# Two conv FFNs with one 512-column matmul for the high half of a weight chunk, matmuls on zeros at the start, and another order of the first loads

## The chip, the cores and the metric

The kernel runs on one core of one Trainium2 chip. The metric is the device time of one execution in microseconds (us). Three runs of the kernel before took 1246.49, 1248.91 and 1246.49 us; the median is 1246.49 us. The execution that was profiled took 1248.71 us.

## The reference, cut to what matters

Two blocks run one after the other on 256 tokens of width 1024, in float32, with one batch row. The first block has two SwiGLU FFNs (width 2816) around a mixer and a gated embedding at its end; the second has two layers, each a mixer and a convolutional FFN. The change bears on the two convolutional FFNs:

```
def conv_ffn(u, w_up, conv_w, conv_b, w_down):
    hdn = causal_dwconv(u @ w_up, conv_w) + conv_b
    gate, val = jnp.split(hdn, 2, axis=-1)
    return (jax.nn.silu(gate) * val) @ w_down
```

Here `w_up` is 1024 x 5632, `w_down` is 2816 x 1024, and the convolution is causal over three tokens and separate for each channel. The norms before and after it, the mixers and the first block stay as they are.

## The kernel before, in words

**Arithmetic.** Every large product is made from three products in the fp32r format. A weight `raw` that DMA has brought is split into `hi` (ScalarE, a copy that rounds) and `lo` (VectorE, the difference of `raw` and `hi`); the activations are split in the same way into `xh` and `xl`. The product is `hi*xh + hi*xl + lo*xh`, added up in PSUM.

**Tiling.** Weights come in halves of a chunk, 128 x 1024 values (512 KB) each, through three `raw` buffers and six `hi` and six `lo` buffers (`halves`, lines 584 to 606). An FFN has 11 groups of 256 inner channels. The up product of nearly all groups is made by `row_units` (line 713): the weight is the stationary operand and the moving one is the activations of all 256 tokens, 8 steps of 128 inner rows for each half of a chunk. In a convolutional FFN the first group of a layer goes another way (`col_units`); the other ten have two chunks each, of two halves: ten groups x 2 x 2 x 8 is 320 steps in a layer, 640 in both. The two halves of a chunk (gate and value channels) share one PSUM bank of 512 columns. The down product of a group takes the weights as the moving operand, 512 columns at a time, and adds up in four banks that stay in use over the whole layer. So four of the eight PSUM banks are left for the up products.

**What follows an up product** (`up_fin`, line 1627): ScalarE scales each half from PSUM and adds the bias, VectorE adds the two shifted taps straight from PSUM, then ScalarE makes the silu, GpSimd the product, and ScalarE and VectorE split it for the down product.

**Order.** The code first records all operations (`Plan`, lines 67 to 371) and then lists them with a planner, which lays them out in time by a table of assumed costs: forward passes place operations by priority, and a backward pass between two forward passes makes new priorities. `ITERS` is the number of forward passes, of which the one with the shortest planned end is used; `bias` moves an operation's priority by hand, and `LB` says how much of that is kept for the later passes. Every engine then works off its list in that order. All DMA goes through SyncE's queue (SP).

The steps of the prediction touch `row_units`, `up_fin`, `halves`, `xt` (line 631), `consts` (line 528) and `run` (line 1691).

Of the kernel before, what the change touches and what calls it, by code (L numbers as in the profile page):

```python
# [14 lines left out]
P = 128  # L15
# [8 lines left out]
LEAD = 2  # L24
RING = 6
# [8 lines left out]
ITERS = 2  # L34
# [6 lines left out]
LB = 0.2  # L41
# [332 lines left out]
class Kern:  # L374
    def __init__(self, plan, a, tap):
        self.plan, self.nc, self.a, self.tap = plan, plan.nc, a, tap
        self.phase = 0
        self.pieces = PIECES

# [48 lines left out]
    def tt(self, out, a, b, op, eng="DVE"):  # L428
        n = self.fsz(out)

        def way(eng):
            if op == ALU.pow:
                c = 360 + 165 * n
            else:
                c = 114 + 2.13 * n if eng == "POOL" else 69 + 1.04 * n + self.part(out)
            return eng, c, lambda: self.ew(eng).tensor_tensor(out=out, in0=a, in1=b, op=op), op != ALU.pow and not self.ps_(a, b)  # L436
        self.plan.add([way(x) for x in eng.split("|")], [out], [a, b])

# [89 lines left out]
    def consts(self):  # L528
# [7 lines left out]
        self.plan.bias = -2e6  # L536
# [47 lines left out]
    def halves(self, src, idx, width, gain_k=None):  # L584

        def prep(h):
# [3 lines left out]
            for j in range(np_):  # L590
                z = slice(j * hw // np_, (j + 1) * hw // np_)
                self.dma(raw[:, z], src[idx][:, h * hw:(h + 1) * hw][:, z])
# [38 lines left out]
    def xt(self):  # L631
        xh = self.plan.tile("xh", [P, KD, S], F32R, 2)
        xl = self.plan.tile("xl", [P, KD, S], F32R, 2)
        return xh, xl
# [77 lines left out]

    def row_units(self, src, c0, xh, xl, fin):

        box = {}
        units = []
        for hf, prep in enumerate(self.halves(src, c0, 2048)):
            def run(prep=prep, hf=hf):
                hi, lo = prep()
                if hf == 0:  # L720
                    box["ps"] = self.psum("m").rearrange("p (c t) -> p c t", c=2)
                o = box["ps"][:, hf, :]
                for k in range(KD):
                    wh, wl = hi[:, 128 * k:128 * k + 128], lo[:, 128 * k:128 * k + 128]
                    self.mms([(o, wh, xh[:, k, :], k == 0, False), (o, wh, xl[:, k, :], False, False),
                              (o, wl, xh[:, k, :], False, k == KD - 1)])
                if hf == 1:
                    fin(box["ps"])
            units.append(run)
        return units  # L730


    def ffn(self, src, na, xh, xl, rs, fin):
# [21 lines left out]
        def row_fin(i):  # L755
            def f(ps):
# [8 lines left out]
                self.tt(gu, ps, rb, ALU.mult)  # L765
# [25 lines left out]
        for g in range(NG + 1):  # L791
            if g < na:
                self.run_units(self.col_units(src, up_at[g], 512, xh, xl, tok_fin(g)))
            elif g < NG:
                for c in range(2):
                    for run in self.row_units(src, up_at[g] + c, xh, xl, row_fin(2 * g + c)):
                        run()
            if g > 0:
                self.run_units(down(g - 1), lead=2 if g == NG else 0)
# [822 lines left out]
    def conv_ffn(self, layer, xh, xl, fin):  # L1622
# [4 lines left out]
        def up_fin(i):  # L1627
            def f(ps):
                tm = self.big("cv").rearrange("p (c t) -> p c t", c=2)
                ws = [lambda j, c=c: cw[:, j, 2 * i + c:2 * i + c + 1] for c in range(2)]  # L1630
                for c, w in enumerate(ws):
                    self.act(tm[:, c], ps[:, c], AF.Identity, bias=w(3), scale=w(2))
                for c, w in enumerate(ws):
                    self.stt(tm[:, c, 1:], ps[:, c, :S - 1], w(1), tm[:, c, 1:], ALU.mult, ALU.add)
                    self.stt(tm[:, c, 2:], ps[:, c, :S - 2], w(0), tm[:, c, 2:], ALU.mult, ALU.add)
# [40 lines left out]
        for g in range(NG + 1):  # L1676
# [3 lines left out]
            elif g < NG:  # L1680
                for i in (2 * g, 2 * g + 1):
                    for run in self.row_units(a[f"cf_u{layer}"], i, xh, xl, up_fin(i)):
                        run()
            if g > 0:
                if g < NG:
                    self.run_units(down(g - 1), lead=0)
                else:
                    self.run_units(down(g - 1), lead=2)


    def run(self):
# [6 lines left out]
        for i in range(4):  # L1698
            for z in ([slice(0, 256), slice(256, 512)] if i == 0 else [slice(0, 512)]):
                self.plan.bias = -1e6 if i == 0 and z.start == 0 else 0  # L1700
# [228 lines left out]
```

## Time and profile before

| | |
|---|---|
| median of three runs | 1246.49 us |
| the profiled execution | 1248.71 us |
| its span (first to last instruction) | 1246.9 us |
| TensorE matmuls busy | 1218.3 us, 8084 instructions |
| VectorE busy | 857.1 us |
| ScalarE busy | 672.4 us |
| GpSimd busy | 194.5 us |

Matmuls are pipelined: each row gives a duration of 0.28 us (256 columns), although the next one starts 0.12 us later. So what a matmul costs is read from the distance of the starts, and a busy TensorE isn't yet one at its peak. The names are output <- moving operand, stationary operand: `psa<-xh,hi` is the high activations against the high weights. Line 513 is the helper that issues nearly all matmuls, 436 and 451 the VectorE helpers, 470 and 477 the ScalarE ones.

### The profile page before, as it was taken

How to read it: one execution, taken by the hardware profiler on the slowest of the kernel's cores; microseconds unless marked ns; L12 is line 12 of the kernel's file. 1: busy time of each engine (PE TensorE's matmuls, PEld its weight loads, DVE VectorE, ACT ScalarE, POOL GpSimd, SP SyncE). 2: the span in 40 equal slices, each digit the busy share in tenths (PEclk: the TensorE clock that was granted, in tenths of full speed). 3: DMA queues.
4: the chain of work that ended last, by engine and by line, in shares of the span. 5: the costliest groups of instructions: out<-in, count | busy, mean ns of one | idle time of the engine just before them, and what ended most of it. 6: DMA issues, size and time to landing. Idle time of an engine off the chain costs nothing.

```text
span 1246.9 us, 21305 instructions
## 1 busy us (share of the span) xinstructions
PE 1218.3 (98%) x8084; PEld 1101.0 (88%) x8084; DVE 857.1 (69%) x1627; ACT 672.4 (54%) x1125; POOL 194.5 (16%) x247
## 2 busy tenths in 40 slices
PE   7999999999999999999999999999999999999997
PEld 7899998787899999789998799999799887999996
DVE  5665567876755655778687786776868557766776
ACT  5444445764654444557465675555652356655554
POOL 2111010420011111002001011111113521111111
PEclk9999999999999999999999999999999999999999
DMA  8755554425455555552424555555553244555552
GB/s 282 231 185 176 189 180 148 143 94 194 161 181 188 187 183 192 180 165 78 146 75 150 195 174 185 181 196 181 187 190 103 80 158 155 185 179 193 187 194 93
DMA packets 61158, 209.61 MB, mean 168 GB/s; under 512 B 7424, under 2 KB 9728, under 8 KB 60928
## 3 DMA queue, kind: packets, MB, share of 16 engines
q1 hardware_dynamic: 61056, 208.26, 50.6%
q8 instruction: 63, 1.03, 0.3%
q14 instruction: 39, 0.32, 0.1%
HBM read 207.18 MB, written 1.05 MB: 167 GB/s over the span
## 4 chain that ended last, share of the span: by engine, by line
PE 79%; DVE 7%; DMA 5%; ACT 4%; issue 2%; POOL 1%; SPq 0%; DVEq 0%; POOLq 0%; ACTq 0%
PE psa L513 77%; DVE lo L436 3%; ACT hi L470 2%; DMA raw<-in_w_ffn 2%; PE psa L524 2%; DVE big L451 1%; DMA raw<-in_cf_u 1%; DVE big L436 1%; POOL sml L436 1%; ACT big L470 1%; DMA raw<-in_w_out 1%; DMA big<-in_xT 1%; ACT L366 1%; DVE xl L436 0%; DVE c_h L451 0%
## 5 line engine op out<-in xcount | busy, mean ns | idle before, releaser
L436 DVE TENSOR_TENSOR lo<-raw,hi 128x512 fp32r<-128x512 f32 x756 | 506.9, 715 | 244.0 <-ACT hi L470 240.7
L470 ACT ACTIVATE hi<-raw 128x1024 fp32r<-128x1024 f32 x381 | 394.0, 1047 | 336.1 <-PE psa L513 237.1
L513 PE MATMUL psa<-xh,hi 128*128 128x256 f32 x1568 | 448.6, 286 | 7.3 <-ACT hi L470 7.0
L513 PE MATMUL psa<-xh,lo 128*128 128x256 f32 x1568 | 445.3, 284 | 1.3 <-DVE lo L436 1.0
L513 PE MATMUL psa<-xl,hi 128*128 128x256 f32 x1568 | 443.7, 283 | 0.1
L513 PEld LDWEIGHTS psa<-xh,hi 128*128 128x128 f32 x1568 | 298.8, 191 | 16.8 <-ACT hi L470 7.4
L513 PEld LDWEIGHTS psa<-xl,hi 128*128 128x128 f32 x1568 | 298.6, 190 | 9.5 <-DVE xl L436 0.4
L513 PEld LDWEIGHTS psa<-xh,lo 128*128 128x128 f32 x1568 | 298.4, 190 | 3.2 <-DVE lo L436 3.1
L513 PE MATMUL psa<-hi,halfr 128*128 128x512 f32 x720 | 212.0, 395 | 0.5 <-DVE halfr L436 0.4
L436 POOL TENSOR_TENSOR big<-big 128x256 f32<-128x256 f32 (+1 forms) x88 | 90.6, 1031 | 597.3 <-ACT big L470 513.0
L513 PE MATMUL psa<-hi,xh 128*128 128x512 f32 (+1 forms) x368 | 144.4, 411 | 2.2 <-ACT xh L470 1.6
L513 PE MATMUL psa<-lo,xh 128*128 128x512 f32 (+1 forms) x368 | 137.5, 392 | 0.9 <-DVE lo L436 0.8
L513 PE MATMUL psa<-hi,xl 128*128 128x512 f32 (+1 forms) x368 | 135.9, 410 | 2.3 <-DVE xl L436 2.2
L513 PEld LDWEIGHTS psa<-hi,halfr 128*128 128x128 f32 x720 | 121.9, 188 | 15.5 <-DVE halfr L436 1.0
L513 PE MATMUL psa<-lo,halfr 128*128 128x512 f32 x360 | 113.6, 391 | 0.5 <-DVE lo L436 0.5
L513 PE MATMUL psa<-big,big 128*128 128x128 f32 (+8 forms) x652 | 92.9, 274 | 1.3 <-DVE big L436 0.9
L513 PEld LDWEIGHTS psa<-big,big 128*128 128x128 f32 (+6 forms) x652 | 86.8, 188 | 8.2 <-POOL big L436 1.5
L513 PEld LDWEIGHTS psa<-hi,xh 128*128 128x128 f32 x368 | 69.2, 190 | 17.0 <-ACT xh L470 4.9
L513 PEld LDWEIGHTS psa<-lo,xh 128*128 128x128 f32 x368 | 69.7, 189 | 15.0 <-DVE lo L436 3.1
L513 PEld LDWEIGHTS psa<-hi,xl 128*128 128x128 f32 x368 | 68.4, 190 | 16.1 <-DVE xl L436 5.1
L513 PEld LDWEIGHTS psa<-lo,halfr 128*128 128x128 f32 x360 | 67.6, 188 | 16.3 <-DVE lo L436 0.9
L470 ACT ACTIVATE big<-big 128x256 f32<-128x256 f32 (+2 forms) x104 | 45.4, 439 | 59.0 <-DVE big L436 35.2
(167 smaller groups left out, 950.2 us busy)
## 6 DMA issues: line engine op xcount, KB each, us to landing
raw<-in_w_ffn SPq DMA_DIRECT2D x131, 512.0 KB, 4.5
raw<-in_cf_u SPq DMA_DIRECT2D x88, 512.0 KB, 4.2
raw<-in_cf_d SPq DMA_DIRECT2D x44, 512.0 KB, 4.3
raw<-in_w_in SPq DMA_DIRECT2D x16, 512.0 KB, 4.6
raw<-in_w_abB SPq DMA_DIRECT2D x16, 512.0 KB, 3.8
raw<-in_w_cA SPq DMA_DIRECT2D x16, 512.0 KB, 3.9
raw<-in_w_cB SPq DMA_DIRECT2D x16, 512.0 KB, 3.8
raw<-in_w_abA SPq DMA_DIRECT2D x12, 512.0 KB, 4.1
```

The source lines that it names most:

```text
L366: self.nc.scalar.preload_act_table_set(i)
L436: return eng, c, lambda: self.ew(eng).tensor_tensor(out=out, in0=a, in1=b, op=op), op != ALU.pow and not self.ps_(a, b)
L451: lambda: self.nc.vector.scalar_tensor_tensor(out=out, in0=a, scalar=s, in1=b, op0=op0, op1=op1, accum_out=accum),
L470: self.plan.add([("ACT", c, lambda: self.nc.scalar.activation(out, a, f, scale=scale, **kw))], outs, ins, SETS.get(f))
L513: return [self.nc.tensor.matmul(o, l, r, start=st, stop=sp) for o, l, r, st, sp in lst]
L524: self.plan.add([("PE", 4 + P / 1.2, lambda: self.nc.tensor.transpose(out, a, idn))], [out], [a, idn], cols=P * 2)
```

## The change

In the convolutional FFNs `row_wide` takes the place of `row_units` (`WC` is 1; `WF`, the same for the other FFNs, is 0). `xh` and `xl` now lie side by side in one tile, so that a step's high weights meet both in one matmul of 512 columns; the low weights meet `xh` in one of 256 columns. The left half of the bank then holds `hi*xh + lo*xh` and the right half `hi*xl`, so a half of a chunk fills a whole bank. The new `addh` brings the right half to SBUF (ScalarE) and adds it to the left (VectorE, back into PSUM); it is called twice for every chunk, 80 times in all. Eleven matmuls on a tile of zeros (`WARM`) are added at the start, the priorities of the first loads are changed, and `ITERS` goes from 2 to 3 and `LB` from 0.2 to 0. With `ENDG` 1 and `ENDLEAD` 2 the end of an FFN has the same units in the same order as before.

```
+WARM = 11
+WF, WC = 0, 1
-ITERS = 2
+ITERS = 3
-LB = 0.2
+LB = 0.0
...
+    def addh(self, out, ps):
+
+        x = self.half("ph")
+        self.act(x, ps[:, S:], AF.Copy)
+        self.tt(out, ps[:, :S], x, ALU.add)
...
-        self.plan.bias = -2e6
+
+        if WARM:
+            z = self.junk("DVE")
+            self.mset(z, 0.0)
+            ps = self.psum()
+            for _ in range(WARM):
+                self.mm(ps, z[:, :P], z)
+        self.plan.bias = -0.5e6
         self.gT = ld("gT", [P, 4, KD])
...
             for j in range(np_):
+                self.plan.bias = -1e6 if np_ > 1 and j == 0 else self.plan.bias if np_ == 1 else 0
                 z = slice(j * hw // np_, (j + 1) * hw // np_)
...
-        xh = self.plan.tile("xh", [P, KD, S], F32R, 2)
-        xl = self.plan.tile("xl", [P, KD, S], F32R, 2)
-        return xh, xl
+
+        x = self.plan.tile("x2", [P, KD, 2, S], F32R, 2)
+        self.both[x.tensor.name] = x
+        return x[:, :, 0], x[:, :, 1]
...
+    def row_wide(self, src, c0, xh, fin):
+
+
+        x2 = self.both[xh.tensor.name]
+        box = {}
+        units = []
+        for hf, prep in enumerate(self.halves(src, c0, 2048)):
+            def run(prep=prep, hf=hf):
+                hi, lo = prep()
+                ps = self.psum("m")
+                o = ps[:, :S]
+                for k in range(KD):
+                    wh, wl = hi[:, 128 * k:128 * k + 128], lo[:, 128 * k:128 * k + 128]
+                    self.mms([(ps, wh, x2[:, k].rearrange("p a t -> p (a t)"), k == 0, False),
+                              (o, wl, x2[:, k, 0], False, k == KD - 1)])
+                box[hf] = ps
+                if hf == 1:
+                    fin([box[0], box[1]])
+            units.append(run)
+        return units
...
+                if isinstance(ps, list):
+                    for x in ps:
+                        self.addh(x[:, :S], x)
+                    x = [x[:, :S] for x in ps]
+                else:
+                    x = [ps[:, c] for c in range(2)]
                 for c, w in enumerate(ws):
-                    self.act(tm[:, c], ps[:, c], AF.Identity, bias=w(3), scale=w(2))
+                    self.act(tm[:, c], x[c], AF.Identity, bias=w(3), scale=w(2))
...
-                    for run in self.row_units(a[f"cf_u{layer}"], i, xh, xl, up_fin(i)):
+                    for run in (self.row_wide(a[f"cf_u{layer}"], i, xh, up_fin(i)) if WC else
+                                self.row_units(a[f"cf_u{layer}"], i, xh, xl, up_fin(i))):
                         run()
...
-                self.plan.bias = -1e6 if i == 0 and z.start == 0 else 0
+                self.plan.bias = -0.6e6 if i == 0 and z.start == 0 else 0
```

SyncE's queue at the start of the program. Of `raw` and `in_w_ffn` (first FFN's weights) 128x256 is a quarter of a half chunk, `in_xT` are the activations, `in_gT` the gains. Before:

```order
L494 DMA c_gT_61<-in_gT 128x32
L494 DMA big_89<-in_xT 128x256
L494 DMA raw_114<-in_w_ffn 128x1024
L494 DMA raw_102<-in_w_ffn 128x256 x2
L494 DMA big_90<-in_xT 128x512
L494 DMA big_89<-in_xT 128x256
L494 DMA raw_106<-in_w_ffn 128x1024
L494 DMA big_91<-in_xT 128x512
L494 DMA raw_102<-in_w_ffn 128x256 x2
L494 DMA big_92<-in_xT 128x512
L494 DMA c_h_86<-in_x 128x2048
```

and now:

```order
L505 DMA raw_102<-in_w_ffn 128x256
L505 DMA big_90<-in_xT 128x256
L505 DMA c_gT_63<-in_gT 128x32
L505 DMA raw_114<-in_w_ffn 128x1024
L505 DMA raw_102<-in_w_ffn 128x256
L505 DMA big_91<-in_xT 128x512
L505 DMA big_90<-in_xT 128x256
L505 DMA big_92<-in_xT 128x512
L505 DMA raw_102<-in_w_ffn 128x256 x2
L505 DMA big_93<-in_xT 128x512
L505 DMA raw_106<-in_w_ffn 128x1024
L505 DMA c_h_88<-in_x 128x2048
```

One quarter of the weights of `raw_102` is now the first load of all, `raw_114` goes from third to fourth, and `raw_106` from ahead of the last two loads of activations to behind them. TensorE's list begins now with eight of the matmuls on zeros (the last of them stands at the head here), two steps of the first FFN, and the other three:

```order
L524 MATMUL psa_62<-junkDVE_61 128x512
L524 MATMUL psa_117<-x_0_89,hi_115 128x256 x2
L524 MATMUL psa_117<-x_0_89,lo_116 128x256
L524 MATMUL psa_105<-x_0_89,hi_103 128x256 x2
L524 MATMUL psa_105<-x_0_89,lo_104 128x256
L524 LDWEIGHTS junkDVE_61
```

The zeros are written by GpSimd, behind all its other clearing at the start.

In the second convolutional FFN, TensorE before (`xh`, `xl` the activations, `halfr` the stationary operand of the down product):

```order
L513 MATMUL psa_135<-xh_87,hi_118 128x256
L513 MATMUL psa_135<-xl_88,hi_118 128x256
L513 MATMUL psa_135<-xh_87,lo_104 128x256
L513 MATMUL psa_136<-hi_123,halfr_129 128x512
L513 MATMUL psa_131<-hi_123,halfr_129 128x512
```

and now (`x_0` holds both halves):

```order
L524 MATMUL psa_131<-x_0_89,hi_107 128x512
L524 MATMUL psa_131<-x_0_89,lo_104 128x256
L524 MATMUL psa_105<-hi_118,halfr_129 128x512
L524 MATMUL psa_136<-hi_118,halfr_129 128x512
L524 MATMUL psa_105<-lo_124,halfr_129 128x512
L524 MATMUL psa_136<-lo_124,halfr_129 128x512
```

Three rows of a step are now two, and the steps stand among the same rows of the down product. VectorE's list in the same FFN has the two additions into PSUM (`psa_131`, `psa_125`) in it, ahead of the two halves of a `lo` and of the taps that read the sum:

```order
L441 TENSOR_TENSOR psa_131<-psa_131,half_171 128x256
L441 TENSOR_TENSOR psa_125<-psa_125,half_168 128x256
L441 TENSOR_TENSOR lo_116<-raw_106,hi_103 128x512 x2
L441 TENSOR_TENSOR halfr_113<-big_141,halfr_134 128x256
L462 SCALAR_TENSOR_TENSOR big_142<-psa_131,c_cf_w_0_81,big_142 128x255
L462 SCALAR_TENSOR_TENSOR big_142<-psa_125,c_cf_w_0_81,big_142 128x255
L462 SCALAR_TENSOR_TENSOR big_142<-psa_131,c_cf_w_0_81,big_142 128x254
L462 SCALAR_TENSOR_TENSOR big_142<-psa_125,c_cf_w_0_81,big_142 128x254
L441 TENSOR_TENSOR lo_119<-raw_102,hi_107 128x512 x2
```

A chunk now has two banks (`psa_131` and `psa_125`), the next chunk the other two (`psa_109` and `psa_62`).

## Rows read from the trace of the kernel before

**Rows 1.** The page's busy times of each engine: us, share, instructions.
```profile
PE 1218.3 (98%) x8084; PEld 1101.0 (88%) x8084; DVE 857.1 (69%) x1627; ACT 672.4 (54%) x1125; POOL 194.5 (16%) x247
```

**Rows 2.** Stretches: length, busy PE, PEld, DVE, ACT, POOL, granted clock, DMA share, GB/s.
```profile
6.80:14.60 7.80, 7.35 (x29) 6.54 (x30) 6.83 (x16) 3.79 (x8) 0.00 (x0) 1.00 1.01 376
14.60:58.50 43.90, 42.77 (x326) 40.23 (x324) 28.27 (x47) 24.31 (x39) 9.28 (x14) 1.00 0.77 251
790.00:870.00 80.00, 79.92 (x566) 74.88 (x566) 56.03 (x102) 44.11 (x67) 10.73 (x10) 1.00 0.57 188
...
888.50:900.00 11.50, 9.38 (x39) 6.78 (x40) 9.90 (x18) 6.51 (x15) 2.28 (x3) 0.85 0.48 147
...
1080.00:1200.00 120.00, 120.00 (x849) 112.35 (x848) 86.64 (x160) 66.28 (x102) 17.45 (x15) 1.00 0.55 184
1237.50:1246.90 9.40, 2.96 (x14) 2.11 (x12) 5.55 (x10) 2.75 (x8) 1.10 (x2) 0.81 0.30 112
```

**Rows 3.** Timeline of TensorE in the second conv FFN: start, duration, instruction.
```profile
1075.00 0.28 PE L513 MATMUL psa<-xh,hi 128*128 128x256 f32 x1
...
1082.47 0.62 PE L513 MATMUL psa<-hi,halfr 128*128 128x512 f32 x2
...
1083.38 0.28 PE L513 MATMUL psa<-xh,hi 128*128 128x256 f32 x1
```

**Rows 4.** The same timeline, a later stretch.
```profile
1109.93 0.28 PE L513 MATMUL psa<-xh,hi 128*128 128x256 f32 x1
...
1113.54 0.64 PE L513 MATMUL psa<-hi,halfr 128*128 128x512 f32 x2
...
1120.37 0.63 PE L513 MATMUL psa<-hi,halfr 128*128 128x512 f32 x2
...
1121.30 0.28 PE L513 MATMUL psa<-xh,hi 128*128 128x256 f32 x1
```

**Rows 5.** Timeline of all engines at the start.
```profile
1.72 1.91 POOL L491 MEMSET big<- 128x512 f32 x4
...
3.56 0.11 POOL L491 MEMSET c_phalf<- 128x16 f32 x1
...
5.69 1.67 ACT L470 ACTIVATE hi<-raw 128x1024 fp32r<-128x1024 f32 x3 [1.46 <-DMA raw<-in_w_ffn]
...
6.80 0.58 PE L513 MATMUL psa<-xh,hi 128*128 128x256 f32 x1 [6.80 <-ACT hi L470]
...
14.21 0.41 PE L513 MATMUL psa<-xh,hi 128*128 128x256 f32 x1
14.42 0.34 PE L513 MATMUL psa<-xl,hi 128*128 128x256 f32 x1
14.60 0.28 PE L513 MATMUL psa<-xh,lo 128*128 128x256 f32 x1
```

**Rows 6.** Chain of waits, in order of time: start, us, what.
```profile
50.91 5.37 DMA raw<-in_w_ffn
58.50 129.74 PE psa L513 x914
```

**Rows 7.** Timeline of TensorE after the first conv FFN.
```profile
890.14 1.32 PE L524 MATMUL psa<-c_ident,big 128*128 128x128 f32 x8 [1.65 <-DVE big L451]
...
894.12 0.63 PE L513 MATMUL psa<-hi,xl 128*128 128x512 f32 x1
894.54 0.63 PE L513 MATMUL psa<-hi,xh 128*128 128x512 f32 x1
```

**Rows 8.** Groups by shape, whole span: line, instruction, count, us, mean ns.
```profile
L436 DVE TENSOR_TENSOR big<-big,psa 128x256 f32<-128x256 f32 x18 | 7.4, 414 | 5.3 <-PE psa L513 4.9 <-ACT big L470 0.2
L477 ACT ACTIVATE big<-psa 128x256 f32<-128x256 f32 x11 | 3.9, 376 | 0.7 <-PE psa L524 0.5
```

**Rows 9.** Timeline of the end.
```profile
1229.86 1.54 PE L513 MATMUL psa<-hi,halfr 128*128 128x512 f32 x6
...
1234.84 0.42 DVE L436 TENSOR_TENSOR halfr<-big,halfr 128x256 fp32r<-128x256 f32 x1 [1.09 <-ACT halfr L470]
```

More of the change, by code (lines that the diff above doesn't have):

```diff
@@ L24 @@
 LEAD = 2
+WARM = 11
+ENDG = 1
+ENDLEAD = 2
+WF, WC = 0, 1
 RING = 6
@@ L378, in __init__ @@
         self.pieces = PIECES
+        self.both = {}
     def big(self, s="b"):
@@ L764, in f @@
                 gu = self.big("gu").rearrange("p (c t) -> p c t", c=2)
-                self.tt(gu, ps, rb, ALU.mult)
+                if isinstance(ps, list):
+                    for c in range(2):
+                        self.addh(gu[:, c], ps[c])
+                    self.tt(gu, gu, rb, ALU.mult)
+                else:
+                    self.tt(gu, ps, rb, ALU.mult)
                 self.act(gu[:, 0], gu[:, 0], AF.Silu)
@@ L795, in ffn @@
                 for c in range(2):
-                    for run in self.row_units(src, up_at[g] + c, xh, xl, row_fin(2 * g + c)):
+                    for run in (self.row_wide(src, up_at[g] + c, xh, row_fin(2 * g + c)) if WF else
+                                self.row_units(src, up_at[g] + c, xh, xl, row_fin(2 * g + c))):
                         run()
-            if g > 0:
-                self.run_units(down(g - 1), lead=2 if g == NG else 0)
+            if 0 < g < NG + 1 - ENDG:
+                self.run_units(down(g - 1), lead=0)
+            elif g == NG:
+                self.run_units([u for i in range(NG - ENDG, NG) for u in down(i)], lead=ENDLEAD)
     def add_half(self, t, acc):
@@ L1630, in f @@
                 ws = [lambda j, c=c: cw[:, j, 2 * i + c:2 * i + c + 1] for c in range(2)]
+                if isinstance(ps, list):
+                    for x in ps:
+                        self.addh(x[:, :S], x)
+                    x = [x[:, :S] for x in ps]
+                else:
+                    x = [ps[:, c] for c in range(2)]
                 for c, w in enumerate(ws):
-                    self.act(tm[:, c], ps[:, c], AF.Identity, bias=w(3), scale=w(2))
+                    self.act(tm[:, c], x[c], AF.Identity, bias=w(3), scale=w(2))
                 for c, w in enumerate(ws):
-                    self.stt(tm[:, c, 1:], ps[:, c, :S - 1], w(1), tm[:, c, 1:], ALU.mult, ALU.add)
-                    self.stt(tm[:, c, 2:], ps[:, c, :S - 2], w(0), tm[:, c, 2:], ALU.mult, ALU.add)
+                    self.stt(tm[:, c, 1:], x[c][:, :S - 1], w(1), tm[:, c, 1:], ALU.mult, ALU.add)
+                    self.stt(tm[:, c, 2:], x[c][:, :S - 2], w(0), tm[:, c, 2:], ALU.mult, ALU.add)
                 self.act(tm[:, 0], tm[:, 0], AF.Silu)
@@ L1681, in conv_ffn @@
                 for i in (2 * g, 2 * g + 1):
-                    for run in self.row_units(a[f"cf_u{layer}"], i, xh, xl, up_fin(i)):
+                    for run in (self.row_wide(a[f"cf_u{layer}"], i, xh, up_fin(i)) if WC else
+                                self.row_units(a[f"cf_u{layer}"], i, xh, xl, up_fin(i))):
                         run()
[L1684 to L1688, printed above, removed]
+            if 0 < g < NG + 1 - ENDG:
+                self.run_units(down(g - 1), lead=0)
+            elif g == NG:
+                self.run_units([u for i in range(NG - ENDG, NG) for u in down(i)], lead=ENDLEAD)
     def run(self):
```

## The prediction

> **What bounds the kernel now.** First the page's busy times: TensorE is busy for 98% of the span, VectorE for 69%, ScalarE for 54% [rows 1]. That alone doesn't say that TensorE sets the end, so next come the stretches. In the second convolutional FFN TensorE has no idle time at all in 120 us (1080 to 1200), in the first it is busy for 79.92 of 80 us (790 to 870); VectorE is busy there for 72% and 70%, ScalarE for 55%, and DMA for a little over half [rows 2]. So there the number of matmuls and the distance of their starts set the time, and nothing else does. The chain of waits says the same for all but the first part: it runs through DMA loads of weights until 58.5, and from there through 914 matmuls in one piece [rows 6]. Over the span TensorE is idle for 1246.9 - 1218.3 = 28.6 us: 6.8 before the first matmul [rows 5], 6.4 at the end (9.4 - 2.96) [rows 2], and some 15 us in small pieces between. One of these is dearer than it looks: after 1.65 us of idle time at 888.5 the granted clock of that stretch is 0.85 [rows 2, 7], and 512-column matmuls start 0.42 us apart [rows 7], the lower of the two levels (1.2 GHz).
>
> **The step of three matmuls becomes two.** What one costs is the distance of the starts. From 1075.00 to 1082.47 there are 63 matmuls of 256 columns: 0.1186 us each. From there to 1083.38 there are four of 512: 0.2275 each [rows 3]. A little later, with the two kinds mixed, 30 of 256 take 1109.93 to 1113.54, 0.1203 each, and four of 512 take 0.93 us, 0.2325 each [rows 4]. So 512 columns cost nearly twice what 256 do, and a step saves only what two of 256 cost above one of 512: 2 x 0.1186 - 0.2275 = 9.7 ns, or 2 x 0.1203 - 0.2325 = 8.1 ns. Nothing of the arithmetic goes: 768 columns are streamed before and after. Middle value 8.9 ns, times 640 steps (320 in each layer): **-5.7 us**, all of it on the path, since TensorE has no idle time there.
>
> A 512 that alternates with a 256 on other weights isn't in the trace. The bounds come from crossing the two stretches: best 0.2275 + 0.1186 against a dear triple of 0.3609, 14.8 ns or -9.5 us; worst 0.2325 + 0.1203 against a cheap triple of 0.3558, 3.0 ns or -1.9 us. I keep the middle, as in both stretches each kind was read beside the other.
>
> The Trainium skill has a rule that speaks against this: by "TensorE: Matmul & The Clock Gate", section "Wait — 56ns, not 53.3ns?", a matmul at the full clock takes its columns and a fixed 2.5 ns, so one matmul less would save 2.5 ns a step, an estimated 1.6 us in all. The trace shows 8 to 10 ns and decides; the sum by the page would be 4.1 us higher.
>
> **What is added for it.** Each of the 80 calls of `addh` is a ScalarE copy of 128x256 from PSUM and a VectorE addition with one operand in PSUM. The nearest rows are 0.376 and 0.414 us [rows 8]: 30.1 us of ScalarE and 33.1 us of VectorE, half in each layer. A layer's steady part is about 160 us, so VectorE goes from 72% to some 82%, ScalarE from 55% to some 64%. TensorE's full queue covers both: 0 us. If that cover is gone, each addition in front of a `lo` that TensorE waits for costs 0.41 us. The copy waits for the last matmul of its half, and behind it on ScalarE stand the next `hi`; the addition waits for the copy, and behind it on VectorE stand the next two `lo` and the taps, and TensorE needs both `hi` and `lo`. The lists are written ahead with these costs in them, and six `hi` and `lo` buffers lie between, so I take 0, and -0 to +13 as bounds (32 of 80 additions late).
>
> PSUM also gets tighter: a chunk holds two banks, from its first matmul to its last tap, so two chunks fit into the four free banks and not four. One chunk of matmuls and its share of the down product last about 16 x 0.353 + 12 x 0.232 = 8.4 us, so a pair of banks comes round every 17 us, of which the matmuls of its chunk take 6 to 9. What has to be done before release (copy, addition, scaling, two taps for each half, among the `lo`) took about 4 us without the new parts and is 5 to 6 with them. It fits; 0 us, in the bounds above.
>
> At the end of an FFN the last chunk's chain is bare. Before, the last up matmul is followed by 28 of the down product before one needs the last chunk: 28 x 0.23 = 6.4 us, and the chain took 1235.26 - 1229.86 = 5.4 us [rows 9]. Now 32 stand there, 7.4 us, and the chain grows by copy, addition and their hand-overs to 6.4 to 6.8 us. Still covered: 0, at most +1.5 for both layers.
>
> **The start.** Before, the first matmul comes at 6.80, when the first `hi` is there, and until 14.6 they start 0.21 us apart (lower level), 29 of them; then 0.12 [rows 2, 5]. At the upper level these 29 would take 29 x 0.09 = 2.6 us less: the most there is to gain. (The granted-clock column says 1.00 here; the distances tell the level.) GpSimd finishes its clearing at 3.67 [rows 5] and then writes the zeros, 0.1 to 0.5 us by its small and its 512-column rows. So TensorE starts at about 4.0, and eight matmuls at 0.42 [rows 7] last until about 7.5: the first real one comes 0.7 us later than now. The load of `raw_114`, which it needs, moves from third to fourth place, so it would not start at 6.80 anyhow. Three more on zeros cost up to 1.3 us. The clock rose 7.7 us after the first matmul at the start, which had gaps, and about 5 us after the restart at 890.14 [rows 5, 7]; from 4.0 that makes 9 to 11.7. After that the remaining 23 of the 29 take 0.12 each, and TensorE could be up to 2 us ahead by 14.6.
>
> But it is then fed by the loads: until 58.5 the chain is DMA, and TensorE's idle time from 14.6 to 58.5 is only 1.1 us [rows 2, 6], which means that it keeps pace with the weights; being ahead turns into waiting. DMA is full from 6.8 to 14.6 (share 1.01) and at 0.77 after, so the new order of the loads mostly exchanges places: activations 512 KB earlier, `raw_106` behind them. I let a third of the 2 us stay: **-0.7 us**, bounds -2.6 (all of it) and +2.1 (the zeros push the first steps back and the clock rises no earlier).
>
> **The other order elsewhere.** Three passes and `LB` 0 rearrange the mixers slightly: the same work, with transposes and weight products exchanged. Of the 15 us of small gaps some will close and others open. One like that at 888.5 is worth 1.65 us and ten matmuls x 0.2, 3.7 us. Nothing says which; 0, bounds -4 and +4.
>
> **Sum.** 1248.7 (the profiled execution; span 1246.9 and 1.8 around it) - 5.7 - 0.7 = 1242.3. That execution was 2.2 us above the median of the three shown, so against the median it is 1246.5 - 6.4 = **1240.1 us**. What a measurement here can tell from no change is 0.2%, 2.5 us: faster is below 1244.0, slower above 1249.0.
>
> **Rivals.**
> - *VectorE becomes the bound in the two layers (slower, 0.11).* The 80 additions go ahead of `lo` halves that TensorE then waits for. Price 0.414 us each: the gain is gone from 16 late ones on, slower begins at 22 (22 x 0.414 - 6.4 = +2.7), and with 32 it is 13.2 - 6.4 = +6.8: 1253.3. For it: VectorE at 82% in a fixed order, with fewer free banks to make up for delays. Against it: not a moment of idle TensorE in 120 us with VectorE at 72%.
> - *The saved part isn't there (same, 0.21).* The pair costs 3 ns less than the triple: -1.9, and the start gives nothing because the loads set it: 1244.6. For it: the worst crossing of rows 3 and 4, and the chain at the start. A new gap of 3.7 us elsewhere ends in the same band: 1243.8. Against it: in each stretch alone the difference is 8 or more.
> - *The new order closes gaps as well (faster, 0.13).* The gap at 888.5 with its slow matmuls goes: 1240.1 - 3.7 = 1236.4. For it: 15 us of gaps are there to be had. Against it: the planner doesn't see the waits as they are on the chip, and gaps open as easily.
> - *The forecast itself, 0.55.*
>
> **How the numbers follow.** The first and third case are faster, 0.13 + 0.55 = 0.68; within 0.2% 0.21; slower 0.11. The range should leave out no more than 2 in 10: below, the best crossing with a closed gap is 1246.5 - 9.5 - 0.7 - 2 = 1234; above, the second rival as a whole and nothing of the first: 1248. The forecast's own range is 1237 to 1243.5.
>
> **What would show it.** In the convolutional FFNs 512 on high weights followed by 256 on low ones should take 0.346 to 0.353 us for the pair and TensorE should stay without idle time; a wait of TensorE for VectorE's `lo` or for a bank (its first matmul of a chunk waiting for a tap) would show the first rival. At the start the distance should fall from 0.21 to 0.12 before 12 us, with TensorE waiting for `hi` between there and 58. The forecast is wrong if the stretch between 60 us and the end, the two layers aside, is longer or shorter by more than 3 us.

## The result, and the profile after

The changed kernel takes **1255.3 us** (median of four runs, 1255.26 to 1257.62), the kernel before 1246.5 us beside it: a ratio of 1.0063, interval 1.0046 to 1.0081. It is slower by some 8 us; 1240.1 was forecast, and the result lies above the upper end of the range, 1248.

The page's busy times after, which answer to [rows 1]:

```profile
PE 1220.9 (97%) x7455; PEld 1068.8 (85%) x7455; DVE 883.7 (71%) x1707; ACT 694.7 (55%) x1203; POOL 184.3 (15%) x248
```

There are 629 matmuls fewer (640 of the steps, less the zeros), and yet TensorE is busy 2.6 us longer, in a span of 1253.5 us for 1246.9. So neither the saving nor the loss stands in this line. Where they lie is told by cutting both spans at the same places of the program: VectorE's last addition to the residual `c_h` in each stage. Two of these places in the kernel after (start, duration, instruction; each row holds the last two additions, and the last starts 0.66 us after the first), the ends of the second mixer and of the first convolutional FFN:

```profile
703.82 1.41 DVE L462 SCALAR_TENSOR_TENSOR c_h<-big,sml,c_h 128x512 f32<-128x512 f32 x2
...
901.79 1.41 DVE L462 SCALAR_TENSOR_TENSOR c_h<-big,sml,c_h 128x512 f32<-128x512 f32 x2
```

The stretches between these places, first of the kernel before (stretch, length, busy TensorE and its instructions, granted clock, DMA share, GB/s): first FFN, first mixer, second FFN with what follows it, per-layer part and second mixer, first convolutional FFN, third mixer, second convolutional FFN with the end.

```profile
0.00:207.63 207.63, 198.87 (x1359) 1.00 0.63 204
207.63:323.58 115.95, 113.64 (x617) 1.00 0.42 140
323.58:536.93 213.35, 211.30 (x1394) 1.00 0.56 182
536.93:697.83 160.90, 158.85 (x1106) 1.00 0.37 123
697.83:893.19 195.36, 192.49 (x1296) 1.00 0.57 186
893.19:1051.93 158.74, 154.93 (x1034) 0.99 0.42 140
1051.93:1246.90 194.97, 188.26 (x1285) 0.99 0.52 173
```

The same stretches after:

```profile
0.00:206.96 206.96, 200.70 (x1367) 1.00 0.63 204
206.96:323.04 116.08, 111.77 (x606) 0.99 0.42 136
323.04:543.07 220.03, 217.02 (x1408) 0.99 0.55 178
543.07:704.48 161.41, 158.03 (x1107) 1.00 0.39 127
704.48:902.45 197.97, 192.78 (x976) 1.00 0.57 184
902.45:1060.86 158.41, 154.52 (x1034) 0.99 0.44 140
1060.86:1253.50 192.64, 186.09 (x965) 1.00 0.53 172
```

The differences are -0.7, +0.1, **+6.7**, +0.5, **+2.6**, -0.3 and **-2.3**, in all +6.6 us. The last stretch gained nearly what was forecast for a layer (-2.85). The first convolutional FFN, with the same change, lost. And most of the loss shows in the second FFN, where no matmul was changed, only the order of the lists. Not all of it arose there: in the new order the first mixer's stretch has 11 matmuls fewer and the second FFN's 14 more, so below the two are taken together.

**The second FFN.** There the second `hi` of a chunk comes late. TensorE after (the idle time ahead of an instruction and what ended it stand in brackets):

```profile
348.10 0.28 PE L524 MATMUL psa<-x,lo 128*128 128x256 f32 x1
349.72 0.50 PE L524 MATMUL psa<-x,hi 128*128 128x256 f32 x2 [1.34 <-ACT hi L481]
...
352.19 0.63 PE L524 MATMUL psa<-x,hi 128*128 128x256 f32 x2
352.62 0.41 PE L524 MATMUL psa<-x,lo 128*128 128x256 f32 x1
352.83 0.63 PE L524 MATMUL psa<-x,hi 128*128 128x256 f32 x2
```

and ScalarE, which makes that `hi`:

```profile
348.61 1.06 ACT L481 ACTIVATE hi<-raw 128x1024 fp32r<-128x1024 f32 x1 [2.24 <-DMA raw<-in_w_ffn]
```

TensorE stands for 1.34 us, since ScalarE waited 2.24 us for the load. From 351 to 354.6 the 256-column matmuls then start 0.21 us apart (352.19 to 352.83 for three) and not 0.12: the lower level, 1.2 GHz. The same happens at 252, after waits of 0.95 and 1.48 us. The granted clock of both places:

```profile
252.00:256.00 4.00, 4.00 (x17) 0.57 0.61 166
350.50:355.00 4.50, 4.50 (x25) 0.62 0.59 182
```

The kernel before, once at the upper level, has no such stretch ahead of the one of [rows 7], at 891.8. Over the first mixer and the second FFN together the kernel after is 6.8 us longer: its idle time (length less busy, of the two rows) is 7.32 us for 4.36, 3.0 more, and two times 3.4 us at 0.21 for 0.12 lose about 2.9. The latter is what the distances give in this execution. The three others, with a mean granted clock of 0.996 to 0.998 against 0.995 here, took no less (spans of 1253.5 to 1255.8), so what the lower level costs the median isn't shown.

**The first convolutional FFN.** TensorE's dearest waits there, after, beside the ones at the two ends of the layer that the kernel before has too:

```profile
740.44 0.72 PE L524 MATMUL psa<-hi,halfr 128*128 128x512 f32 x2 [0.59 <-ACT halfr L481]
...
748.78 0.47 PE L524 MATMUL psa<-x,hi 128*128 128x512 f32 x1 [0.77 <-DVE big L462]
...
753.27 0.47 PE L524 MATMUL psa<-x,hi 128*128 128x512 f32 x1 [0.55 <-DVE big L462]
```

and VectorE just before the second of them:

```profile
745.99 1.41 DVE L441 TENSOR_TENSOR psa<-psa,half 128x256 f32<-128x256 f32 x4
747.31 0.41 DVE L441 TENSOR_TENSOR halfr<-big,halfr 128x256 fp32r<-128x256 f32 x1
747.65 0.99 DVE L462 SCALAR_TENSOR_TENSOR big<-psa,c_cf_w,big 128x255 f32<-128x255 f32 x2
748.55 1.28 DVE L441 TENSOR_TENSOR lo<-raw,hi 128x512 fp32r<-128x512 f32 x2
```

The first wait is for the stationary operand of the first down matmul. The other two are for banks: a chunk's first matmul waits for a tap (L462) of an earlier chunk, and this tap stood behind four of the new additions. The kernel before has no wait of either kind there; over 0.4 us it has only one at each end of the layer, 0.45 at 697.31 and the 1.65 of [rows 7].

**The second convolutional FFN** runs without idle time from 1099 to 1219, as before in its steady part [rows 2]:

```profile
1099.00:1219.00 120.00, 120.00 (x629) 1.00 0.58 185
```

Its pattern repeats with each group of two chunks, so the price of a step can be read over three groups. Before, and after:

```profile
1160.22 0.28 PE L513 MATMUL psa<-xh,hi 128*128 128x256 f32 x1
...
1211.22 0.28 PE L513 MATMUL psa<-xh,hi 128*128 128x256 f32 x1
```

```profile
1151.61 0.40 PE L524 MATMUL psa<-x,hi 128*128 128x512 f32 x1
1151.85 0.27 PE L524 MATMUL psa<-x,lo 128*128 128x256 f32 x1
1151.96 0.39 PE L524 MATMUL psa<-x,hi 128*128 128x512 f32 x1
...
1202.16 0.40 PE L524 MATMUL psa<-x,hi 128*128 128x512 f32 x1
```

51.00 / 3 = 17.00 us a group before and 50.55 / 3 = 16.85 after, with 32 steps in each: 4.7 ns a step. Over the whole layer, the distances to the next start added up over all 960 (640) matmuls less the idle times over 0.15 us, a step takes 358.5 ns before and 353.6 after, 4.9 ns less; in the first layer 364.6 and 363.0, 1.6 less. A pair takes 0.350 (1151.61 to 1151.96), 0.23 to 0.24 of it the 512.

### The profile page after: what moved, and what is told of

Same layout as the page of the kernel before. It is cut to its first block, busy times and chain, and to the rows that moved or that the text cites. A ratio compares the mean times of both kernels' runs of the same rounds, so it can differ in the third digit from the quotient of the medians.

```text
span 1253.5 us, 20212 instructions
## 1 busy us (share of the span) xinstructions
PE 1220.9 (97%) x7455; PEld 1068.8 (85%) x7455; DVE 883.7 (71%) x1707; ACT 694.7 (55%) x1203; POOL 184.3 (15%) x248
## 4 chain that ended last, share of the span: by engine, by line
PE 76%; DMA 8%; DVE 8%; ACT 5%; issue 2%; POOL 1%; SPq 0%; DVEq 0%; POOLq 0%; ACTq 0%
PE psa L524 73%; DVE lo L441 4%; DMA raw<-in_cf_u 4%; ACT hi L481 3%; DMA raw<-in_w_ffn 3%; PE psa L535 2%; DVE big L462 1%; DVE big L441 1%; POOL sml L441 1%; DMA raw<-in_w_out 1%; ACT big L481 0%; DMA raw<-in_w_in 0%; DMA raw<-in_cf_d 0%; DVE big L495 0%; DMA raw<-in_w_ple 0%
## 5 line engine op out<-in xcount | busy, mean ns | idle before, releaser
L524 PE MATMUL psa<-x,hi 128*128 128x256 f32 (+1 forms) x2496 | 577.0, 314 | 4.2 <-ACT hi L481 2.8
L481 ACT ACTIVATE hi<-raw 128x1024 fp32r<-128x1024 f32 (+1 forms) x381 | 394.6, 1046 | 306.6 <-PE psa L524 210.9
L524 PEld LDWEIGHTS psa<-x,hi 128*128 128x128 f32 x2496 | 416.8, 190 | 45.6 <-ACT hi L481 5.5
L524 PE MATMUL psa<-x,lo 128*128 128x256 f32 x1568 | 445.7, 284 | 3.1 <-DVE lo L441 2.8
L524 PEld LDWEIGHTS psa<-x,lo 128*128 128x128 f32 x1568 | 297.7, 190 | 13.1 <-DVE lo L441 9.7
L524 PE MATMUL psa<-hi,x 128*128 128x512 f32 (+1 forms) x736 | 247.9, 410 | 4.7 <-DVE x L441 1.8
L524 PEld LDWEIGHTS psa<-hi,x 128*128 128x128 f32 x736 | 134.4, 190 | 31.8 <-DVE x L441 4.4
L524 PE MATMUL psa<-lo,x 128*128 128x512 f32 (+1 forms) x368 | 137.7, 392 | 0.3 <-DVE lo L441 0.2
L524 PEld LDWEIGHTS psa<-lo,x 128*128 128x128 f32 x368 | 69.9, 190 | 14.4 <-DVE lo L441 2.6
L462 DVE SCALAR_TENSOR_TENSOR big<-psa,c_cf_w,big 128x255 f32<-128x255 f32 (+1 forms) x160 | 73.0, 477 | 8.7 <-ACT big L481 7.4
```

Source lines behind the costliest of these rows:

```text
L462: lambda: self.nc.vector.scalar_tensor_tensor(out=out, in0=a, scalar=s, in1=b, op0=op0, op1=op1, accum_out=accum),
L481: self.plan.add([("ACT", c, lambda: self.nc.scalar.activation(out, a, f, scale=scale, **kw))], outs, ins, SETS.get(f))
L524: return [self.nc.tensor.matmul(o, l, r, start=st, stop=sp) for o, l, r, st, sp in lst]
```

## The experiments

All stage times are read as above, by the start of the last addition, from one profiled execution each; that execution can be some us off the median (narrow_work: 1253.1 for 1256.8). "First part" is the end of the second mixer less 697.83, that of the kernel before; the layers are the two convolutional FFNs, each from the end of the mixer ahead of it to its last addition to the residual. The ratio is to the kernel before on the same chip.

| kernel | median us | ratio (95%) | first part | layer 0 | layer 1 |
|---|---|---|---|---|---|
| before | 1246.5 | 1 | 0 | 195.4 | 191.3 |
| after | 1255.3 | 1.0063 (1.0046 to 1.0081) | +6.7 | 198.0 | 189.0 |
| wide_alone | 1251.8 | 1.0033 (1.0020 to 1.0046) | +0.2 | 199.7 | 190.7 |
| after_lb02 | 1265.0 | 1.0141 (1.0124 to 1.0157) | +7.3 | 203.3 | 190.5 |
| before_lb0 | 1252.7 | 1.0042 (1.0030 to 1.0053) | +4.9 | 195.1 | 190.6 |
| after_narrow | 1250.7 | 1.0029 (1.0014 to 1.0043) | +3.6 | 194.0 | 191.3 |
| narrow_noise1 | 1250.7 | 1.0035 (1.0022 to 1.0048) | +1.2 | 196.3 | 192.8 |
| narrow_noise2 | 1251.6 | 1.0040 (1.0027 to 1.0053) | -0.4 | 195.3 | 195.4 |
| wide_noise1 | 1257.4 | 1.0079 (1.0065 to 1.0094) | +2.7 | 202.9 | 189.1 |
| wide_noise2 | 1256.4 | 1.0074 (1.0058 to 1.0089) | +3.5 | 204.1 | 189.6 |
| wide_layer1 | 1249.1 | 0.9995 (0.9982 to 1.0008) | +2.7 | 195.6 | 190.3 |
| wide_sbuf | 1249.6 | 1.0001 (0.9987 to 1.0014) | +1.7 | 198.1 | 191.4 |
| wide_late_down | 1252.0 | 1.0014 (1.0001 to 1.0026) | -1.4 | 200.1 | 190.8 |
| narrow_work | 1256.8 | 1.0052 (1.0032 to 1.0073) | -2.4 | 199.5 | 194.4 |
| wide_no_add | 1245.9 | 0.9997 (0.9985 to 1.0009) | -1.8 | 194.7 | 190.3 |
| wide_no_add_noise1 | 1250.3 | 1.0030 (1.0017 to 1.0042) | +2.4 | 195.3 | 190.2 |
| narrow_work_noise1 | 1256.4 | 1.0071 (1.0055 to 1.0087) | +1.7 | 197.6 | 195.5 |
| wide_sbuf_noise1 | 1254.3 | 1.0053 (1.0037 to 1.0068) | +1.4 | 198.4 | 190.4 |
| wide_lb0 | 1252.5 | 1.0022 (1.0010 to 1.0034) | +4.3 | 199.7 | 188.8 |
| after_sbuf | 1256.2 | 1.0051 (1.0036 to 1.0065) | +4.5 | 199.5 | 189.6 |

The median of the kernel before was 1246.4 to 1250.4 beside these runs; compare by the ratios.

### The parts one by one

The change has three parts that can be had apart: the wide matmuls, the start (zeros, first loads), and the planner's settings.

**wide_alone**, the kernel after with the other parts undone:

```diff
-WARM = 11
+WARM = 0
-ITERS = 3
+ITERS = 2
-LB = 0.0
+LB = 0.2
```

and the three priorities of the first loads as before.

> The kernel before with the wide matmuls of the two convolutional FFNs alone (two for three, the additions, the joined activations); the start, the passes and LB as before. Theory A (the new order of the lists, from LB 0, loses the time; the wide matmul does what was forecast): -5.7 us, about 1241, TensorE idle in the first convolutional FFN no longer than before. Theory B (the wide matmul loses it: two banks for each chunk and the additions make TensorE wait): 1249 to 1255, with waits of TensorE for a tap in front of a chunk's first matmul. Theory C (any new plan moves the time by some us up or down): anywhere from 1238 to 1252.

Measured 1.0033: theory A falls. The wide matmul alone, with the old settings, loses 4.3 us in layer 0, while everything ahead of it takes as long as before. The wait is that for `halfr`:

```profile
736.29 0.73 PE L524 MATMUL psa<-hi,halfr 128*128 128x512 f32 x2 [1.78 <-ACT halfr L481]
```

ScalarE shows why it is late: two `hi` of 1.1 us each stand ahead of that `halfr` in its list.

```profile
732.91 0.42 ACT L481 ACTIVATE big<-big 128x256 f32<-128x256 f32 x1
733.24 0.59 ACT L481 ACTIVATE big<-big,c_cf_w 128x256 f32<-128x256 f32 x1
733.73 2.20 ACT L481 ACTIVATE hi<-raw 128x1024 fp32r<-128x1024 f32 x2
735.84 0.40 ACT L481 ACTIVATE halfr<-big 128x256 fp32r<-128x256 f32 x1
```

**after_lb02** (in the kernel after, `ITERS = 2`, `LB = 0.2`).

> The kernel after with LB and the number of passes as before (0.2, 2). Theory A: the 7 us at the second FFN's entry and the 5 us in the first convolutional FFN come back: 1241 to 1244. Theory B: the 5 us in the first convolutional FFN stay, and the time is 1250 or more. Theory C: neither pattern.

Measured 1.0141, the slowest of all; theory A is out. The first mixer now loses 5.8 us and layer 0 eight, more than half of these in one wait:

```profile
745.58 1.22 PE L524 MATMUL psa<-hi,halfr 128*128 128x512 f32 x2 [4.41 <-ACT halfr L481]
```

**before_lb0** (in the kernel before, `LB = 0.0`).

> The kernel before with LB 0 alone (a third pass changes nothing in its lists). Theory A: slower by what the order loses, 1253 to 1259, with the late entry into the second FFN. Theory B: as before, 1245 to 1248. Theory C: between 1240 and 1258, the gaps elsewhere than in the kernel after.

Measured 1.0042: +4.9 us, all of it in the first part; layer 0 is as before. So the setting costs something by itself, without the rest of the change.

**after_narrow** (in the kernel after, `WF, WC = 0, 0`).

> The kernel after with three matmuls of 256 columns a step again (no wide matmuls, no additions); the zeros, the order of the first loads, LB 0 and three passes stay. Theory A: the gain of 5 us is lost and the order's loss stays: 1258 to 1261. Theory B: 1246 to 1249. Theory C: anywhere from 1244 to 1260.

Measured 1.0029, 1250.7 us: between A and B, nearer to B, and inside C, which is wide. Layer 0, at 194.0, is the quickest of all, so its loss in the kernel after comes from the wide matmul and what goes with it; the first part still loses 3.6.

### Other plans for the same work

Any edit makes the planner draw up new lists for the whole program. What that alone is worth was measured with

```diff
-SEED = 0
-NOISE = 0.0
+SEED = 1
+NOISE = 1.0
```

in the kernel before and in wide_alone (SEED 2 for the second of each).

> The kernel before; its planner gets noise of 1 ns on every priority (NOISE 1, SEED 1), which reorders the lists of all engines among near ties and changes no work. Theory C (any new plan moves the time by some us, and that is most of what was seen): 1240 to 1258, with gaps in other places than before. Theory D (the wide matmul itself brings new waits where a convolutional FFN begins, and a plan alone is worth little): within 3 us of before, 1245 to 1251.

> The same with SEED 2: by theory C 1240 to 1258 and apart from SEED 1 by some us; by theory D 1245 to 1251.

> The wide matmuls alone, with the same noise (NOISE 1, SEED 1). Theory C: 1240 to 1258, no slower than the two noisy kernels with three matmuls a step by more than their spread. Theory D: 1249 to 1256; in the first convolutional FFN TensorE is idle 2.5 to 6 us longer than before, for the halves of the first group (halfr) and for banks.

> The same with SEED 2: theory C 1240 to 1258; theory D 1249 to 1256 with the same idle time in the first convolutional FFN.

Both theories hold in part. A new plan of the kernel before costs 0.35 and 0.40%, some 4 to 5 us, though it does the same work: that is theory C's size. But the wide kernels in the same two plans cost 0.79 and 0.74%, outside the intervals of the others, and the difference stands where theory D puts it: layer 0 takes 202.9 and 204.1 us (196.3 and 195.3 with three matmuls a step), with a wait of 4.48 us for `halfr` in each. Layer 1 gains in both. But theory D's other half, that a plan alone is worth little, falls.

### What in the wide step costs the time

**wide_layer1**:

```diff
-... if WC else
+... if WC and layer == 1 else
```

> Wide matmuls in the second convolutional FFN alone; three a step in the first; start, passes and LB as before. Theory D (the step saves some 2 us a layer; what is lost arises where the first convolutional FFN begins): the second layer takes 189 to 190.7 us (191.3 before), the first 195 to 197 as before; in all 1243 to 1249, the upper part if the new plan costs its 4 us. Theory C (the plan alone): any time from 1244 to 1256, the second layer not systematically shorter.

Measured 0.9995: no difference that can be told. Layer 0 is back at 195.6, layer 1 gains 1.0, and the new plan costs 2.7 us in the first part. Theory D holds.

**wide_sbuf** lets go of the banks earlier:

```diff
-for x in ps:
-    self.addh(x[:, :S], x)
-x = [x[:, :S] for x in ps]
+y = self.big("cs").rearrange("p (c t) -> p c t", c=2)
+for c in range(2):
+    self.addh(y[:, c], ps[c])
+x = [y[:, c] for c in range(2)]
```

> The wide matmuls alone, but the addition writes its sum to SBUF and the taps read it there, so that both banks of a chunk come free after the addition and not after the last tap. Theory D1 (TensorE waits in the first layer since two banks a chunk run out): the first layer falls from 199.7 to 195 to 197, no wait for a tap before a chunk's first matmul, the wait for halfr gone or under 1 us; 1244 to 1249. Theory D2 (the work added on ScalarE and VectorE delays halfr, banks don't matter): the first layer stays at 199 to 204, 1250 to 1257.

Layer 0 falls to 198.1, between D1 and D2. No wait for a tap ahead of a chunk and none for `halfr` over 0.3 us is left; TensorE waits for `hi` and once for `lo` (0.50 us) instead:

```profile
737.08 0.49 PE L524 MATMUL psa<-x,hi 128*128 128x512 f32 x1 [1.18 <-ACT hi L481]
```

**wide_late_down** writes the first group's down product behind the third group's up product:

```diff
-if 0 < g < NG + 1 - ENDG:
-    self.run_units(down(g - 1), lead=0)
+if 1 < g < NG + 1 - ENDG:
+    for i in ([0, 1] if g == 2 else [g - 1]):
+        self.run_units(down(i), lead=0)
```

> The wide matmuls alone, the down product of the first group written after the third group instead of the second, which puts ten more up matmuls between the last transposes and the first down matmul in the list (34 for 24). By theory D1 and D2 alike the wait for halfr (1.78 us) falls by some 1.9 us to 0 or near it; the first layer 197 to 199; 1248 to 1252. If the first layer stays at 199.7 or over, the wait is paid elsewhere.

A miss. The wait for `halfr` at the first down matmul is gone, but layer 0 takes 200.1: the wait is paid for elsewhere, for `hi` and then for a bank.

```profile
733.30 0.49 PE L524 MATMUL psa<-x,hi 128*128 128x512 f32 x1 [1.44 <-ACT hi L481]
...
744.18 0.50 PE L524 MATMUL psa<-x,hi 128*128 128x512 f32 x1 [1.06 <-DVE big L462]
```

Behind the first of these two, from 733.5 to 738.0, the granted clock is 0.62. So the place of the first down matmul alone isn't the cause: `halfr`, `hi` and the taps all come late.

**narrow_work** puts the added work into the kernel before:

```diff
+if i >= 2 * CA:
+    for c in range(2):
+        x = self.half("ph")
+        self.act(x, ps[:, c], AF.Copy, scale=0.0)
+        self.tt(ps[:, c], ps[:, c], x, ALU.add)
```

> The kernel before, three matmuls a step and one bank a chunk, with the 80 ScalarE copies (times 0) and 80 VectorE additions of the wide kernel put into the same place. Theory D1 (banks): first layer 195 to 197, second 191 to 193; 1247 to 1253 with the cost of a new plan. Theory D2 (added work): first layer 199 to 204, 1252 to 1258.

> Three matmuls a step, one bank a chunk, with the added copies and additions, in another plan (NOISE 1, SEED 1). D1: first layer 195 to 197. D2: 198 to 202, as the 199.5 of the first plan.

Layer 0 takes 199.5 and 197.6, layer 1 194.4 and 195.5. In the first plan layer 0 is D2's, in the second it lies between. The work alone, with one bank a chunk and three matmuls a step, slows the layers by 2.2 to 4.2 us against the kernel before; in layer 1 a plan can do as much without it (narrow_noise2: 195.4). Two things differ from the wide kernel. Both halves of a chunk share a bank here, and the second copy waits for the first addition; and the longest wait of layer 0, its end aside, stands well behind the entry, at 808 and 810 us (at 733 to 749 in nine of the ten wide kernels with this work). In narrow_work:

```profile
801.42 0.38 ACT L470 ACTIVATE half<-psa 128x256 f32<-128x256 f32 x1 [0.39 <-DVE psa L436]
...
808.24 0.96 PE L513 MATMUL psa<-hi,halfr 128*128 128x512 f32 x3 [1.39 <-DVE halfr L436]
```

**wide_no_add** is the counterpart: `addh` isn't called (`x = [x[:, :S] for x in ps]` alone), the banks stay as they are. It leaves the product `hi*xl` out of the sum, so it tells of time alone.

> The wide matmuls alone without the copies and additions: the product of the low halves of the activations is computed into the second half of the bank and left out of the sum. Two banks a chunk are held to the last tap as in the wide kernel. Theory D1 (banks): the first layer stays at 198 to 203 us, with waits for a tap or for halfr. Theory D2 (added work): the first layer falls to 193 to 195, the second to 188.5 to 190; 1244 to 1248.

> The same in another plan (NOISE 1, SEED 1), where the kernel with additions took 202.9 us for the first layer. D1: 198 to 203. D2: 193 to 195.5.

Layer 0 takes 194.7 and 195.3; with the same settings the kernel with additions took 199.7 and 202.9. The two banks alone cost nothing; D1 as it stood falls. A wait for `halfr` is still there, but shorter, 0.79 us for 1.78:

```profile
734.81 0.73 PE L524 MATMUL psa<-hi,halfr 128*128 128x512 f32 x2 [0.79 <-ACT halfr L481]
```

> Wide matmuls, sums in SBUF, banks free after the addition, in another plan (NOISE 1, SEED 1). D1: first layer 195 to 198, against 202.9 with the sums in PSUM. D2: 199 to 204.

> The kernel after with the sums of the additions in SBUF, so that both banks come free after the addition. Theory (held banks double what the added work costs): the first convolutional FFN takes 195.5 to 197.8 us (198.0 in the kernel after), no wait for a tap before a chunk; the rest as the plan falls, 1249 to 1256. If it is still 198 or more, the early release is worth nothing in this plan.

With the banks given back early, layer 0 is 198.4 in the noisy plan (202.9 without), just above D1's range, but 199.5 with the settings of the kernel after (198.0 without): a miss. There too no wait for a tap ahead of a chunk is left, but TensorE waits for `hi` (1.11 us) and `lo` (0.53). Put together, layer 0 takes

| | no added work | copies and additions |
|---|---|---|
| one bank, or two given back early | 194.0 to 196.3 (6 kernels) | 197.6 to 199.5 (5) |
| two banks held to the last tap | 194.7, 195.3 | 198.0 to 204.1 (7) |

The column decides. The row matters only beside the added work, and with one of three settings it didn't help. The longest times hold the lower clock behind their waits too: 3.4 us of it in wide_noise1, wide_noise2 and wide_late_down, 6.8 in after_lb02. Each of these edits also draws up new lists, so a single kernel's 1 or 2 us decide nothing; the columns lie apart as wholes.

### LB 0

**wide_lb0** (in wide_alone, `ITERS = 3`, `LB = 0.0`).

> The wide matmuls with LB 0 and three passes, the start as before. If LB 0 as such costs time ahead of the first convolutional FFN: the second mixer ends 3.6 to 6.7 us later than before (697.17), with a wait for hi near 345 us; in all 1252 to 1257. If only the spread of plans is behind it: -2.4 to +3.5 us there, 1248 to 1253. The first convolutional FFN 198 to 204 us either way.

The first part is 4.3 us behind, as the first theory says. Five kernels with `LB` 0 are now 3.6 to 6.7 us behind there (mean 4.8), fourteen others with 0.2 from -2.4 to +7.3 (mean 1.3). All five have a wait of TensorE for `hi` of 0.8 to 1.3 us between 344 and 350 us; no kernel with 0.2 has one of 0.4 us or more there. In before_lb0:

```profile
344.65 0.38 PE L513 MATMUL psa<-xh,hi 128*128 128x256 f32 x1 [0.88 <-ACT hi L470]
```

The second FFN's stretch by itself tells the two settings apart: 216.5 to 220.0 us in the five, 213.1 to 215.0 in the fifteen with 0.2, the kernel before among them. With the first mixer, since work moves between the two, the means are 333.7 and 330.8.

## Why the prediction was wrong

**The step that failed most: "the other order elsewhere ... 0, bounds -4 and +4".** Ahead of the first convolutional FFN the kernel after loses 6.65 us. `LB` weighs a delay that the planner puts on the work of the second half of the tokens; with 0 the loads, the `hi` and the statistics at the entry of the second FFN come in another order, and TensorE waits for a late load. That all five kernels show it, and none of the fifteen others, makes the setting the cause of this delay, worth some 3 us (4.8 less 1.3). The rest is of the size by which plans differ anyway. Why `LB` 0 puts that load late was not followed further, and the 5.8 us of the first mixer in after_lb02 stay open. The prediction's own sign of being wrong, a change of more than 3 us outside the two layers, is there (+6.65 ahead of them, -0.3 between). The bounds were set from single gaps of 3.7 us; the plans made here for unchanged work in that part lie 10 us apart (-2.4 to +7.3). And before counts as a good plan: none of the seven other kernels with three matmuls a step in layer 0 was measurably quicker, and six were slower, the four without added work by 0.29 to 0.42%.

**"Additions 0, bounds 0 to +13": within the bounds, not at the value.** The cover of TensorE's full queue was read in the steady part [rows 2], and there it holds: from 1099 to 1219 TensorE has no idle time with the additions. In the wide kernels the price arises where the first layer begins. There the taps of the first group, the `halfr`, the `hi` of the next chunks and now copies and additions all stand in ScalarE's and VectorE's lists at once, and TensorE has little else to do: in wide_noise2 18 up matmuls lie between the last transposes and the first down matmul in layer 0 (734.0 to 741.9, 4.48 us of it idle), 70 in layer 1 (1079.0 to 1091.4, none idle). Over the seven kernels with two banks held, fewer matmuls there go with a longer wait for the first `halfr`: 18 with 4.41 to 4.48 us (three kernels), 24 with 1.78, 30 with 0.59 and 0.60, 34 with none; layer 1, with 68 to 74, has none. That this is why layer 1 is spared remains a reading: no run changed this number in layer 1, and in narrow_work the longest one comes later. The first rival named this work, and its sign, a chunk's first matmul waiting for a tap, was seen at 748.78 and 753.27. But it put the price on `lo` in the steady part; its time, 1253.3, came near for another reason.

**"PSUM banks 0": right by itself, wrong in company.** Without the added work two banks a chunk cost nothing (194.7, 195.3). With it, giving them back early was worth 1.6 and 4.5 us with two settings and nothing with a third.

**"-5.7 us for the step": the term was mis-sized.** It is 4.9 ns in layer 1 and 1.6 in layer 0, so 320 x 4.9 + 320 x 1.6 = 2.1 us, near the lower bound. The 8.9 ns took the 512-column matmul from eight of the down product (0.2275 and 0.2325, mean 0.230, [rows 3, 4]). The wide one takes 0.2337 on the mean of layer 1 and 0.2410 in layer 0. Of the 3.7 ns by which layer 1 lies above 0.230, 1.7 stand in the sample: all 263 of the down product in that layer take 0.2317 in the kernel before. The other 2.0 come with the wide form or its place. The rest of layer 0's price was not taken apart; idle times under 0.15 us are in it. The mechanism is right all the same: with TensorE never idle, layer 1 gains 4.7 ns a step in three groups. By the Trainium skill, "TensorE: Matmul & The Clock Gate", section "Wait — 56ns, not 53.3ns?", a matmul less was to save 2.5 ns, an estimated 1.6 us in all. The prediction set that aside; the measured sum, 2.1 us, lies nearer to it than to 5.7, though layer 1 alone shows about twice the page's figure.

**"The start -0.7": no gain shown, inside its bounds.** TensorE starts at 4.19 on zeros, and the first real matmul comes at 8.45 (before 6.80, [rows 5]):

```profile
4.19 3.59 PE L524 MATMUL psa<-junkDVE 128*128 128x512 bf16 x8 [4.19 <-POOL junkDVE L502]
8.45 0.80 PE L524 MATMUL psa<-x,hi 128*128 128x256 f32 x2 [0.66 <-ACT hi L481]
...
12.14 0.63 PE L524 MATMUL psa<-x,hi 128*128 128x256 f32 x2
...
12.79 0.60 PE L524 MATMUL psa<-x,hi 128*128 128x256 f32 x2
...
13.35 0.40 PE L524 MATMUL psa<-x,hi 128*128 128x256 f32 x2
...
13.70 0.40 PE L524 MATMUL psa<-x,hi 128*128 128x256 f32 x2
```

Three matmuls take 0.65 us at 12.14 and 0.35 at 13.35; before, the distance fell at about 14.5 [rows 5]. The clock is up 1.3 us sooner, but the work began 1.65 later, and loads set the pace then as before: the chain of waits runs through them until 52.6 (58.5, [rows 6]). The first FFN ends 0.7 us sooner; with the old start it does so too in wide_alone (206.55) and before_lb0 (206.81). Over all kernels it ends at 207.0 to 207.8 with the new start (four) and at 205.8 to 208.4 with the old, so no gain from the start can be told.

**The end: right.** TensorE has no wait for the last chunk's `halfr`, ready at 1241.6.

In the sum: forecast -6.4, measured +6.6 us of span. The 13.0 between them are 7.4 in the first part (+6.65 for -0.7), 5.5 in layer 0 (+2.6 for -2.85), 0.5 in layer 1 with the end (-2.3 for -2.85), and -0.3 in the third mixer.

No version tried that does the whole work beats both kernels. wide_layer1 and wide_sbuf can't be told from the kernel before.

## What to carry to other kernels

Where one planner orders the whole program, a local saving of 2 us is smaller than what drawing up the lists anew does to the rest (here -2.4 to +7.3 us in parts that weren't touched); such a change is judged stage by stage, and over more than one plan. Work moved to engines with spare time is free only where the busy engine has a queue: look at the entry of a stage too, where everyone waits for the first results, and not at the steady part alone. Take a price of some ns from a whole layer and not from eight rows.

## What the runs showed of the hardware

A 512-column matmul costs 0.2317 us from start to start in the down product of the kernel before (mean of 263 in layer 1), 0.2311 there in the kernel after, and 0.2337 as half of a pair in the same layer: the shape gives the price to within 2 or 3 ns. And a short gap can be paid for twice: after 1.34 us of idle time at 348 TensorE ran at 1.2 GHz from 351 to 354.6, which by the distances cost about as much again. It need not be: the waits of 0.77 and 0.55 us at 748 and 753 were not followed by such a stretch, nor the 1.78 us of wide_alone at 736. And the two waits ahead of the stretch at 252 (0.95 and 1.48 us) stand in after_narrow too (0.94 and 1.48), where the granted clock from 252 to 256 is 1.00.
